# One decoder layer, expert part: how the gate matrix is made, and which tiles of product one stay on chip to open product two

## The chip, the cores and the metric

One core of one Trainium2 chip. The metric is the time of one execution in microseconds of device time; lower is better. Arithmetic is float32, where matrix products are made of three products of a value split into a high part (float32r) and a remainder (high times high, high times remainder, remainder times high).

## The reference, cut to what matters

A decoder layer on 512 tokens of width 1024: a mixer (RWKV and dilated attention), and then PEER, a layer of 16384 experts. Only the last part is touched. Per token and head (8 heads) two searches over 128 keys each give 16 best scores `v1, v2` with their key numbers `i1, i2`; the 16 best sums of a pair give 16 experts with softmax gates:

```python
cand = (v1[..., :, None] + v2[..., None, :]).reshape(cshape)          # 16 x 16 sums
cidx = (i1[..., :, None] * 128 + i2[..., None, :]).reshape(cshape)    # expert number
top, sel = lax.top_k(cand, 16);  idx = take_along_axis(cidx, sel)
gate = softmax(top)
act = gelu(einsum('cd,ced->ce', u, peer_u[idx]))                      # product one
out = einsum('ce,ced->cd', gate * act, peer_v[idx])                   # product two
```

## The kernel before, in words

The first 128 tokens (block 0) and the other 384 (blocks 1 to 3) go different ways.

**The 384 tokens** are computed densely. Product one (`phase_peer`, the loop at L1197) runs over 128 tiles `i1` of 128 experts: `gemm_ch` (L145) loads the tile's weights `uT` (512 KB, SP queue), splits them into `whi` (ScalarE, L127) and `wlo` (VectorE, L128), and makes 24 matmuls of 384 columns (L141 to L143); ScalarE applies Gelu (L1203) and the result `act` (128 experts x 384 tokens) is stored to DRAM (L1205, ScalarE's queue), but for the last 8 tiles, which stay on chip in `keep`. There are four pairs of weight buffers (two pools of two), so weights are ready some three tiles ahead.

**The gates** must become a dense matrix G of expert by token. `topk` (L1046) finds candidates, positions (VectorE max, find, replace) and the expert numbers: for each head a comparison, a product and a sum over 16 x 50 elements (L1076 to L1079), with the candidate numbers `cidx` made on GpSimd (L1056); for blocks 1 to 3 the number is then split by shift and mask (L1098 to L1104) and turned by three TensorE transposes into `sl`. `scatter` (L1113) goes through a block in 32 steps of four tokens: a one-hot E for the low part of the number (VectorE, L1122, 512 elements), four one-hots A for the high part times the gate (VectorE, L1126, 128 elements each), four matmuls E by A into one PSUM bank (L1132; the trace shows two passes for each, 8 records a step), and an eviction to `Gs` (ScalarE, L1133). After eight steps `Gs` (2 MB) goes to DRAM (`g_d`, L1135). `routing` (L1170) strings the four yields of one topk and the scatters of three blocks together; the loop of product one takes 10 + (i1 - 9) * 96 / 104 of its steps by tile i1, so that the program has the last of the 106 steps at tile 113; the rest, if any, is run at tile 119, where the pool of the routing (`pp`) is closed and the pool `vg` opened.

**The 128 tokens of block 0** are gathered: `rows_u` (L1144) fetches row after row of `peer_u` by an indirect DMA issued on GpSimd (L1141, 512 KB for 128 tokens, six buffers) and makes the dot product on VectorE (L1150, 1024 elements), one per tile of product one; `rows_v` (L1158) does the same with `peer_v` in product two (VectorE, L1164), into `acc0`.

**Product two** (L1232) runs over the 128 tiles again: the kept ones first, then the others, whose `act` is loaded again (L1243, SP queue). For every eight tiles a slab of G is loaded (L1235, 1.5 MB, from all twelve blocks of `g_d`). Each tile: act times G (VectorE, L1244), high part (ScalarE, L1250), remainder (VectorE, L1251), the weights `v` (512 KB) split as above, 18 matmuls of 512 columns into six PSUM banks. At tile 64 the program loads `h` (2 MB) and `gt2` (0.5 MB) for the end. The last four tiles are gone through output by output, so that the end can be pipelined.

**Order.** The program gives each piece a place by the `yield`s of these generators, but the order of the instructions on each engine is found when the kernel is built, by a scheduler that runs a model of the time (`schedule_with_timeline_sim`): an instruction with a later place in the program can be put ahead, when its inputs and its buffer are free. On the chip each engine, and each DMA queue, keeps the order that it was given.

Of the kernel before, what the change touches and what calls it, by code (L numbers as in the profile page):

```python
# [18 lines left out]
P = 128  # L19
# [25 lines left out]
GI = 8  # L45
# [55 lines left out]
class Kern:  # L101
# [942 lines left out]
    def topk(self, pp, i, res):  # L1044
# [5 lines left out]
        nc.vector.tensor_scalar(xf[:, :, 0], xf[:, :, 0], 128.0, None, op0=OP.mult)  # L1050
        cand = pp.tile([P, 8, NCAND], F32, tag="cand", name="cand")
        cidx = pp.tile([P, 8, NCAND], F32, tag="cidx", name="cidx")
        for p, (o, n) in enumerate(CAND):
            nc.vector.tensor_tensor(cand[:, :, o:o + n], v[:, :, 0, p:p + 1].to_broadcast([P, 8, n]),
                                    v[:, :, 1, 0:n], op=OP.add)
            nc.gpsimd.tensor_tensor(cidx[:, :, o:o + n], xf[:, :, 0, p:p + 1].to_broadcast([P, 8, n]),  # L1056
                                    xf[:, :, 1, 0:n], op=OP.add)
# [15 lines left out]
        xs = pp.tile([P, 8, 16], F32, tag="xs", name="xs")  # L1073
        for h in range(8):
            eq = pp.tile([P, 16, NCAND], F32, tag="eq", name="eq", bufs=2)
            nc.vector.tensor_tensor(eq, self.iota[:, None, :NCAND].to_broadcast([P, 16, NCAND]),  # L1076
                                    posf[:, h, :, None].to_broadcast([P, 16, NCAND]), op=OP.is_equal)
            nc.vector.tensor_tensor(eq, eq, cidx[:, h, None, :].to_broadcast([P, 16, NCAND]), op=OP.mult)
            nc.vector.tensor_reduce(xs[:, h], eq, axis=AX.X, op=OP.add)  # L1079
            if h % 2:  # L1080
                yield
# [8 lines left out]
        if i == 0:  # L1090
            xi = self.gp.tile([P, 8, 16], I32, name="xi0")
            nc.vector.tensor_copy(xi, xs)
# [5 lines left out]
        xi = pp.tile([P, 8, 16], I32, tag="xi", name="xi")  # L1098
        x2 = pp.tile([P, 8, 16], I32, tag="x2", name="x2")
        nc.vector.tensor_copy(xi, xs)  # L1100
        nc.vector.tensor_scalar(x2, xi, 127, None, op0=OP.bitwise_and)
        nc.vector.tensor_copy(sel[:, 1], x2)
        nc.vector.tensor_scalar(x2, xi, 7, None, op0=OP.logical_shift_right)
        nc.vector.tensor_copy(sel[:, 0], x2)  # L1104
# [8 lines left out]
    def scatter(self, pp, i, res):  # L1113

        nc = self.nc
        sl = res[i]
        for t4 in range(0, 128, 4):
            if t4 % GB == 0:
                Gs = pp.tile([P, 128, GB], F32, tag="Gs", name="Gs", bufs=2)
            E = pp.tile([P, 4, 128], F32, tag="ohE", name="ohE", bufs=2)  # L1120
            A = pp.tile([P, 4, 128], F32, tag="ohA", name="ohA", bufs=2)
            nc.vector.tensor_tensor(E, self.iota[:, None, :].to_broadcast([P, 4, 128]),  # L1122
                                    sl[:, 1, t4:t4 + 4, None].to_broadcast([P, 4, 128]), op=OP.is_equal)
            for j in range(4):
                t = t4 + j
                nc.vector.tensor_scalar(A[:, j], self.iota, sl[:, 0, t:t + 1], sl[:, 2, t:t + 1],  # L1126
                                        op0=OP.is_equal, op1=OP.mult)
            o = t4 % GB
            tg = "cdef"[t4 // 4 % 4]
            g = self.psum.tile([P, 4, 128], F32, tag=tg, name="gps", bufs=BANKS[tg])  # L1130
            for j in range(4):
                nc.tensor.matmul(g[:, j], E[:, j], A[:, j], start=True, stop=True)  # L1132
            nc.scalar.activation(Gs[:, :, o:o + 4].rearrange("p i t -> p t i"), g, AF.Copy)  # L1133
            if o == GB - 4:
                nc.scalar.dma_start(self.g_d[((i - 1) * 128 + t4) // GB], Gs)  # L1135
            yield
# [44 lines left out]
    def phase_peer(self, es):  # L1181
# [7 lines left out]
        self.iota = pp.tile([P, 128], F32, name="iota")  # L1189
# [6 lines left out]
        done = 0  # L1196
        for i1 in range(128):  # L1197
# [6 lines left out]
            if i1 < 128 - NR:  # L1204
# [12 lines left out]
        order = list(range(128 - NR, 128)) + list(range(128 - NR))  # L1217
# [4 lines left out]
        rows = self.rows_v(acc0)  # L1222
        LAST = 4
# [8 lines left out]
        for n, i1 in enumerate(order):  # L1232
            if n % GI == 0:
                G = vg.tile([P, TD // GB, GI, GB], F32, tag="G", name="G", bufs=2)
                nc.sync.dma_start(G, self.g_d[:, :, i1:i1 + GI, :].rearrange("b p i t -> p b i t"))  # L1235
# [3 lines left out]
            if i1 in keep:  # L1239
                act = keep[i1]  # L1240
            else:
                act = ap.tile([P, TD], F32, tag="act", name="act", bufs=4)
                nc.sync.dma_start(act, self.act_d[i1])  # L1243
            nc.vector.tensor_tensor(act.rearrange("p (b t) -> p b t", t=GB), act.rearrange("p (b t) -> p b t", t=GB),  # L1244
                                    G[:, :, n % GI, :], op=OP.mult)
            bufs = LAST if n >= 128 - LAST else 3
            tg = "f" if n >= 128 - LAST else ""
            wh = (vp if tg else vg).tile([P, TD], F32R, tag="wh" + tg, name="wh", bufs=bufs)
            wl = (vp if tg else vg).tile([P, TD], F32R, tag="wl" + tg, name="wl", bufs=bufs)
            nc.scalar.activation(wh, act, AF.Copy)  # L1250
            nc.vector.tensor_tensor(wl, act, wh.bitcast(F32), op=OP.subtract)  # L1251
            hi, lo = self.wtile(I["v"][i1 * 128:(i1 + 1) * 128, :])
            ws = (wh, wl, hi, lo)
# [22 lines left out]
def host(inputs):  # L1276
# [44 lines left out]
    a["iota"] = np.tile(np.arange(128, dtype=np.float32), (128, 1))  # L1321
# [17 lines left out]
```

## Time and profile before

| what | us |
|---|---|
| median of three runs (2125.58 to 2130.1) | 2126.97 |
| the profiled execution's own time | 2125.92 |
| its span in the trace | 2124.1 |
| product one with the scatters, in the trace | about 927 to 1561 |
| product two, in the trace | 1582.7 to about 2110 |

The span starts at the first instruction; the execution's own time has 1.8 us around it. TensorE is busy in 95% of the span, VectorE 75%, ScalarE 44%, GpSimd 30%. PEld is TensorE's loading of weights, which runs beside its matmuls. A granted clock of 1.00 is 2.4 GHz, 0.50 would be 1.2 GHz.

### The profile page before, as it was taken

To read this page: it belongs to the slowest core of one execution; us is meant where nothing else is said; L and a number is where in the kernel's file an instruction comes from. 1 tells how busy PE (TensorE), PEld (TensorE's weight loads), DVE (VectorE), ACT (ScalarE), POOL (GpSimd) and SP (SyncE) were. 2 spreads that over 40 slices of the span, in tenths; PEclk is the share of its full clock that TensorE was granted. 3 is DMA by queue.
4 is the path that set the end of the run, shared out by engine and by line. 5 is a ranking of instruction groups with operands and counts; after the bars stand their busy time and mean duration, and the time that the engine had idled before them with its cause. 6 is when DMAs were issued, how large, how long until landed. Compare 5 with 4: busy or idle time off the path is not lost.

```text
span 2124.1 us, 34025 instructions
## 1 busy us (share of the span) xinstructions
PE 2022.2 (95%) x12529; PEld 1744.0 (82%) x12529; DVE 1600.9 (75%) x3192; ACT 935.8 (44%) x1452; POOL 642.8 (30%) x511
## 2 busy tenths in 40 slices
PE   5999899999999998999999999999959999999999
PEld 4677667877877786899998999999958887877887
DVE  7466894853534555899999999987768898988555
ACT  3756665543324443334334454456633333333332
POOL 2424550221402111001674545420015555551000
PEclk9999989998889998999999999999979999999999
DMA  6666855354435532335998999985589999999763
GB/s 260 224 189 201 256 170 149 94 189 147 140 121 173 186 127 72 108 119 173 386 360 293 334 359 349 375 316 203 198 292 358 388 392 398 394 391 344 230 211 110
DMA packets 236299, 519.45 MB, mean 245 GB/s; under 512 B 35554, under 2 KB 129506, under 8 KB 233572
## 3 DMA queue, kind: packets, MB, share of 16 engines
q1 hardware_dynamic: 180260, 334.27, 46.4%
q0 software_dynamic: 36864, 134.23, 16.9%
q10 hardware_dynamic: 19008, 48.77, 6.0%
q8 instruction: 99, 1.62, 0.3%
q14 instruction: 68, 0.56, 0.1%
HBM read 432.23 MB, written 84.97 MB: 243 GB/s over the span
## 4 chain that ended last, share of the span: by engine, by line
PE 65%; DVE 16%; DMA 10%; issue 4%; ACT 3%; POOL 2%; SPq 0%; DVEq 0%; ACTq 0%; POOLq 0%
PE ps_mm L141 13%; PE ps_mm L143 13%; PE ps_mm L142 13%; DVE wlo L128 4%; PE gps L1132 4%; DMA wraw<-in_v 3%; DMA act<-act_d 2%; DVE row L1150 2%; PE yp L735 2%; PE yp L733 2%; PE ps_a L143 1%; PE ps_a L142 1%; PE ps_a L141 1%; DMA wada<-in_wada 1%; DVE acc L1164 1%
## 5 line engine op out<-in xcount | busy, mean ns | idle before, releaser
L127 ACT ACTIVATE whi<-wraw 128x1024 fp32r<-128x1024 f32 x356 | 370.1, 1042 | 388.6 <-PE ps_mm L142 226.9
L128 DVE TENSOR_TENSOR wlo<-wraw,whi 128x1024 fp32r<-128x1024 f32 x356 | 430.4, 1212 | 131.5 <-ACT whi L127 127.8
L141 PE MATMUL ps_mm<-n2h,whi 128*128 128x384 f32 (+1 forms) x1152 | 399.9, 347 | 3.2 <-ACT act L1203 3.2
L142 PE MATMUL ps_mm<-n2l,whi 128*128 128x384 f32 (+1 forms) x1152 | 398.2, 346 | 0.0
L143 PE MATMUL ps_mm<-n2h,wlo 128*128 128x384 f32 (+1 forms) x1152 | 396.1, 345 | 2.1 <-DVE wlo L128 2.1
L1141 POOL DMA_INDIRECT row<-in_v,xi x128 | 196.7, 1537 | 339.7 <-DVE acc L1164 166.5
L1141 POOL DMA_INDIRECT row<-in_u,xi x128 | 187.0, 1461 | 171.3 <-DVE dots L1150 132.7
L141 PEld LDWEIGHTS ps_mm<-n2h,whi 128*128 128x128 f32 x1152 | 218.4, 190 | 9.1 <-ACT act L1203 4.4
L143 PEld LDWEIGHTS ps_mm<-n2h,wlo 128*128 128x128 f32 x1152 | 218.2, 190 | 7.7 <-DVE wlo L128 2.8
L142 PEld LDWEIGHTS ps_mm<-n2l,whi 128*128 128x128 f32 x1152 | 218.3, 190 | 4.7
L141 PE MATMUL ps_mm<-n1h,whi 128*128 128x512 f32 x464 | 193.8, 421 | 8.8 <-ACT n1h L271 5.0
L143 PE MATMUL ps_mm<-n1h,wlo 128*128 128x512 f32 x464 | 192.5, 415 | 1.2 <-DVE wlo L128 1.2
L142 PE MATMUL ps_mm<-n1l,whi 128*128 128x512 f32 x464 | 192.4, 415 | 0.2 <-DVE n1l L272 0.2
L1250 ACT ACTIVATE wh<-act 128x384 fp32r<-128x384 f32 x128 | 66.9, 525 | 279.1 <-DVE act L1244 144.4
L1164 DVE SCALAR_TENSOR_TENSOR acc<-row,g,acc 128x1024 f32<-128x1024 f32 x127 | 162.3, 1278 | 0.8
L1150 DVE CUSTOM_DVE_ANT_0 row<-row,n2t 128x1024 f32<-128x1024 f32 x128 | 153.0, 1218 | 0.0
L1244 DVE TENSOR_TENSOR act<-act,G 128x384 f32<-128x384 f32 x128 | 69.8, 553 | 87.1 <-DMA act<-act_d 72.6
L1133 ACT ACTIVATE Gs<-gps 128x512 f32<-128x512 f32 x96 | 107.1, 1120 | 57.8 <-PE gps L1132 55.8
L141 PE MATMUL ps_mm<-whi,wh 128*128 128x512 f32 x256 | 92.6, 395 | 29.2 <-ACT wh L1250 29.0
L141 PEld LDWEIGHTS ps_mm<-n1h,whi 128*128 128x128 f32 x464 | 91.1, 198 | 32.5 <-ACT n1h L271 5.0
L143 PEld LDWEIGHTS ps_mm<-n1h,wlo 128*128 128x128 f32 x464 | 91.5, 197 | 23.0 <-DVE wlo L128 2.2
L142 PEld LDWEIGHTS ps_mm<-n1l,whi 128*128 128x128 f32 x464 | 92.1, 198 | 21.7 <-issue 2.4
(405 smaller groups left out, 4000.6 us busy)
## 6 DMA issues: line engine op xcount, KB each, us to landing
wraw<-in_uT SPq DMA_DIRECT2D x128, 512.0 KB
wraw<-in_v SPq DMA_DIRECT2D x128, 512.0 KB
wraw<-in_win SPq DMA_DIRECT2D x60, 512.0 KB
g_d<-Gs ACTq DMA_DIRECT2D x12, 2048.0 KB
G<-g_d SPq DMA_DIRECT2D x16, 1536.0 KB
act_d<-act ACTq DMA_DIRECT2D x120, 192.0 KB
act<-act_d SPq DMA_DIRECT2D x120, 192.0 KB
wada<-in_wada SPq DMA_DIRECT2D x64, 256.0 KB
```

What stands on the lines that cost most here:

```text
L127: nc.scalar.activation(hi[:, :n], raw[:, :n], AF.Copy)
L128: nc.vector.tensor_tensor(lo[:, :n], raw[:, :n], hi[:, :n].bitcast(F32), op=OP.subtract)
L141: mm(acc, lh, rh, start=start, stop=False)
L142: mm(acc, lh, rl, start=False, stop=False)
L143: mm(acc, ll, rh, start=False, stop=stop)
L1132: nc.tensor.matmul(g[:, j], E[:, j], A[:, j], start=True, stop=True)
L1133: nc.scalar.activation(Gs[:, :, o:o + 4].rearrange("p i t -> p t i"), g, AF.Copy)
L1141: self.nc.gpsimd.indirect_dma_start(row, None, self.I[tab], bass.IndirectOffsetOnAxis(ap=self.xi[:, n:n + 1], axis=0))
L1150: self.gathered(self.rowp, n, "u", lambda row: nc.vector.tensor_tensor_reduce(out=row, in0=row, in1=self.n2t, scale=1.0, scalar=0.0, op0=O ...
L1164: nc.vector.scalar_tensor_tensor(acc, row, self.gates0[:, n:n + 1], acc, op0=OP.mult, op1=OP.add)
L1244: nc.vector.tensor_tensor(act.rearrange("p (b t) -> p b t", t=GB), act.rearrange("p (b t) -> p b t", t=GB), G[:, :, n % GI, :], op=OP.mult)
L1250: nc.scalar.activation(wh, act, AF.Copy)
```

## The change

Four things in the expert part:

- **Gates into one-hots on ScalarE.** One comparison makes both one-hots A and E of a step (1024 elements, VectorE), and the four products of A with the gate are made by ScalarE (an ACTIVATE of 128 elements with the gate as a scale per partition). The one-hots have three buffers for two.
- **Indices by row and column.** The position in the list of 50 candidates is turned into a row (a sum of steps `dx` between row numbers, over comparisons with the 16 row offsets) and a column (position minus row offset), for two heads at a time, on 32 x 16 elements. `cidx` and GpSimd's part in it fall away, as do shift and mask; the table `iota` has the offsets and their differences behind its 128 numbers.
- **Scatter paced to end sooner** (96 / 98 steps a tile for 96 / 104, closing at tile 112 for 119), and 7 gathered rows of `rows_u` in 8 tiles for one a tile; the other 16 come in the first 17 tiles of product two, and `rows_v` after them, at 1.28 a tile.
- **The first 8 tiles stay on chip** and product two takes the tiles in their order. The first slab of G is loaded at tile 112 of product one, and three of the kept tiles are weighed (times G, split) at tiles 120, 122 and 124. The outputs go in the order of banks (2, 3, 1).

```diff
-        nc.vector.tensor_scalar(xf[:, :, 0], xf[:, :, 0], 128.0, None, op0=OP.mult)
+        dx = pp.tile([P, 8, 16], F32, tag="dx", name="dx")
+        nc.vector.tensor_copy(dx[:, :, 0:1], xf[:, :, 0, 0:1])
+        nc.vector.tensor_tensor(dx[:, :, 1:], xf[:, :, 0, 1:], xf[:, :, 0, :15], op=OP.subtract)
...
-            nc.gpsimd.tensor_tensor(cidx[:, :, o:o + n], xf[:, :, 0, p:p + 1].to_broadcast([P, 8, n]),
-                                    xf[:, :, 1, 0:n], op=OP.add)
...
-        for h in range(8):
-            eq = pp.tile([P, 16, NCAND], F32, tag="eq", name="eq", bufs=2)
-            nc.vector.tensor_tensor(eq, ..., op=OP.is_equal)
-            nc.vector.tensor_tensor(eq, eq, cidx[:, h, None, :].to_broadcast([P, 16, NCAND]), op=OP.mult)
-            nc.vector.tensor_reduce(xs[:, h], eq, axis=AX.X, op=OP.add)
+        for h0 in range(0, 8, 2):
...
+            nc.vector.tensor_tensor(ge, ph[:, :, None].to_broadcast([P, n, 16]), row(128), op=OP.is_ge)
+            nc.vector.tensor_tensor(by_head(eq), by_head(ge), dx[:, hs, None, :].to_broadcast([P, 2, 16, 16]), op=OP.mult)
+            nc.vector.tensor_reduce(sel[:, 0, hs].rearrange("p h k -> p (h k)"), eq, axis=AX.X, op=OP.add)
+            nc.vector.tensor_tensor(ge, ge, row(144), op=OP.mult)
+            off = pp.tile([P, n], F32, tag="off", name="off", bufs=2)
+            nc.vector.tensor_reduce(off, ge, axis=AX.X, op=OP.add)
+            nc.vector.tensor_tensor(off, ph, off, op=OP.subtract)
+            nc.vector.tensor_tensor(eq, off[:, :, None].to_broadcast([P, n, 16]), row(0), op=OP.is_equal)
+            nc.vector.tensor_tensor(by_head(eq), by_head(eq), xf[:, hs, 1, None, :].to_broadcast([P, 2, 16, 16]), op=OP.mult)
+            nc.vector.tensor_reduce(sel[:, 1, hs].rearrange("p h k -> p (h k)"), eq, axis=AX.X, op=OP.add)
+            yield
...
-            E = pp.tile([P, 4, 128], F32, tag="ohE", name="ohE", bufs=2)
-            A = pp.tile([P, 4, 128], F32, tag="ohA", name="ohA", bufs=2)
-            nc.vector.tensor_tensor(E, ..., op=OP.is_equal)
+            AE = pp.tile([P, 2, 4, 128], F32, tag="ohAE", name="ohAE", bufs=3)
+            A, E = AE[:, 0], AE[:, 1]
+            nc.vector.tensor_tensor(AE, self.iota[:, None, None, :128].to_broadcast([P, 2, 4, 128]),
+                                    sl[:, 0:2, t4:t4 + 4, None].to_broadcast([P, 2, 4, 128]), op=OP.is_equal)
             for j in range(4):
-                nc.vector.tensor_scalar(A[:, j], self.iota, sl[:, 0, t:t + 1], sl[:, 2, t:t + 1],
-                                        op0=OP.is_equal, op1=OP.mult)
+                nc.scalar.activation(A[:, j], A[:, j], AF.Copy, scale=sl[:, 2, t:t + 1])
...
+        def load_g(i1):
+            G = Gs[i1] = vg.tile([P, TD // GB, GI, GB], F32, tag="G", name="G", bufs=2)
+            nc.sync.dma_start(G, self.g_d[:, :, i1:i1 + GI, :].rearrange("b p i t -> p b i t"))
+        def weigh(i1, act):
+            nc.vector.tensor_tensor(act..., act..., Gs[i1 - i1 % GI][:, :, i1 % GI, :], op=OP.mult)
...
+            nc.scalar.activation(wh, act, AF.Copy)
+            nc.vector.tensor_tensor(wl, act, wh.bitcast(F32), op=OP.subtract)
+            ready[i1] = wh, wl
...
-            if i1 < 128 - NR:
+            if i1 >= NR:
                 act = ap.tile([P, TD], F32, tag="act", name="act", bufs=4)
...
-            next(rows, None)
-            while done < min(i1 + 1, 10) + max(i1 - 9, 0) * 96 // 104:
+            if i1 % 8 < 7:
+                next(rows, None)
+            while done < min(i1 + 1, 10) + max(i1 - 9, 0) * 96 // 98:
...
-            if i1 == 119:
+            if i1 == 112:
                 run(bg)
                 e1.close()
                 vg = self.pool(es, "vg")
-        run(rows)
+                load_g(0)
+            elif i1 >= 120 and i1 % 2 == 0 and len(ready) < 3:
+                weigh(len(ready), keep[len(ready)])
...
-        order = list(range(128 - NR, 128)) + list(range(128 - NR))
...
-                for t in out:
+                for t in (2, 3, 1):
...
-            next(rows, None)
-            if n > 64:
-                next(rows, None) if n % 16 == 0 else None
-        run(rows)
+            if n < 17:
+                next(rows, None)
+            while vdone < max(n - 16, 0) * 128 // 100:
+                next(rows_v, None)
+                vdone += 1
+        run(rows_v)
```

## Rows read from the trace of the kernel before

**Rows 1.** The profile's page, its first part: busy time, share of the span and count of instructions of each engine.
```profile
PE 2022.2 (95%) x12529; PEld 1744.0 (82%) x12529; DVE 1600.9 (75%) x3192; ACT 935.8 (44%) x1452; POOL 642.8 (30%) x511
```
**Rows 2.** Busy time by stage: the stretch, its length, busy time (and instructions) of PE, PEld, DVE, ACT, POOL, the granted clock, the DMA engines' share and GB/s.
```profile
1119.00:1407.00 288.00, 283.23 (x1721) 281.81 (x1720) 281.44 (x575) 136.02 (x167) 135.59 (x103) 0.98 0.94 344
1407.00:1561.00 154.00, 152.16 (x1028) 151.75 (x1026) 118.11 (x289) 94.78 (x105) 2.61 (x2) 1.00 0.59 209
1561.00:1582.00 21.00, 0.10 (x1) 0.00 (x0) 6.33 (x6) 1.07 (x1) 5.84 (x5) 0.55 0.97 347
1582.00:2110.00 528.00, 519.48 (x2265) 427.17 (x2266) 420.24 (x507) 188.53 (x252) 182.49 (x117) 0.99 0.90 329
```
**Rows 3.** The same view, 40 us of product one ahead of the scatters, and twice 40 us of product two.
```profile
1000.00:1040.00 40.00, 40.00 (x232) 40.00 (x232) 40.00 (x117) 13.55 (x19) 27.26 (x31) 1.00 0.92 339
1600.00:1640.00 40.00, 40.00 (x178) 33.11 (x177) 35.99 (x40) 14.78 (x20) 20.61 (x16) 1.00 0.96 351
...
1840.00:1880.00 40.00, 36.37 (x154) 29.61 (x153) 33.86 (x40) 13.31 (x17) 20.46 (x13) 0.96 1.04 395
```
**Rows 4.** The chain that ended last, between the two products: start, length, what.
```profile
1561.14 1.08 ACT Gs L1133
1562.24 7.40 DMA g_d<-Gs
1569.72 11.81 DMA G<-g_d
1581.56 0.57 DVE act L1244
1582.15 0.53 ACT wh L1250
```
**Rows 5.** PE in order of time at the same place: start, length, engine, line, what, and in brackets the idle time ahead and what ended it.
```profile
1559.93 1.17 PE L1132 MATMUL gps<-ohA,ohE 128*128 128x128 f32 x8 [1.60 <-DVE ohA L1126]
1582.73 0.80 PE L141 MATMUL ps_mm<-whi,wh 128*128 128x512 f32 x1 [21.63 <-ACT wh L1250]
...
1587.10 0.40 PE L141 MATMUL ps_d<-whi,wh 128*128 128x512 f32 x1
```
**Rows 6.** PE in order of time: the first matmul of a tile of product one, one of the two steps of the scatter inside this tile, and the first matmul of the next tile.
```profile
1480.26 0.42 PE L141 MATMUL ps_mm<-n2h,whi 128*128 128x384 f32 x1
...
1484.16 1.05 PE L1132 MATMUL gps<-ohA,ohE 128*128 128x128 f32 x8
...
...
1486.21 0.42 PE L141 MATMUL ps_mm<-n2h,whi 128*128 128x384 f32 x1
```
**Rows 7.** DVE by line from 927 to 1561: line, operation, names, shapes, count, busy us, mean ns, idle time ahead.
```profile
L1150 DVE CUSTOM_DVE_ANT_0 row<-row,n2t 128x1024 f32<-128x1024 f32 x128 | 153.0, 1218 | 0.0
L1126 DVE TENSOR_SCALAR ohA<-iota,sl 128x128 f32<-128x128 f32 x384 | 106.7, 344 | 0.0
L1122 DVE TENSOR_TENSOR ohE<-iota,sl 128x512 f32<-128x512 f32 x96 | 65.8, 685 | 8.9 <-PE gps L1132 8.8
L1076 DVE TENSOR_TENSOR eq<-iota,posf 128x800 f32<-128x800 f32 x32 | 31.0, 981 | 0.0
```
**Rows 8.** DVE in order of time: two 1024-element operations in a row, and two steps of the scatter.
```profile
1107.57 2.35 DVE L128 TENSOR_TENSOR wlo<-wraw,whi 128x1024 fp32r<-128x1024 f32 x2
...
1545.33 0.69 DVE L1122 TENSOR_TENSOR ohE<-iota,sl 128x512 f32<-128x512 f32 x1
...
1546.96 0.69 DVE L1122 TENSOR_TENSOR ohE<-iota,sl 128x512 f32<-128x512 f32 x1
```
**Rows 9.** Busy time by stretch of the scatter's PSUM tile alone: PE, PEld and ACT (eight PE records, and one eviction, are a step).
```profile
1000.00:1400.00 400.00, 43.28 (x328) 42.53 (x328) 46.27 (x41) 0.99 0.94 347
1400.00:1556.00 156.00, 54.68 (x418) 53.97 (x419) 56.71 (x51) 1.00 0.62 223
```
**Rows 10.** Busy time by stretch of line 1203 alone (the Gelu of product one, one a tile, and five table loads).
```profile
920.00:1400.00 480.00, 55.26 (x106) 0.99 0.87 315
```
**Rows 11.** ACT by line from 927 to 1561, columns as in the DVE rows.
```profile
L127 ACT ACTIVATE whi<-wraw 128x1024 fp32r<-128x1024 f32 x128 | 135.2, 1063 | 174.7 <-PE ps_mm L142 139.6 <-DMA wraw<-in_uT 16.0 <-ACT act L1203 5.0
L1133 ACT ACTIVATE Gs<-gps 128x512 f32<-128x512 f32 x95 | 106.0, 1121 | 56.1 <-PE gps L1132 54.1
L1203 ACT ACTIVATE act<-ps_mm 128x384 f32<-128x384 f32 x128 | 61.8, 482 | 91.5 <-PE ps_mm L143 85.1 <-issue 3.7 <-DMA wraw<-in_uT 2.8
...
L1085 ACT ACTIVATE sel<-sel 128x128 f32<-128x128 f32 x4 | 1.2, 311 | 3.0 <-DVE sel L1084 3.0
```
**Rows 12.** ACT in order of time, at a place of the merge: an ACTIVATE of 512 elements with a constant as its scale, and one of the same size with a scale per partition.
```profile
794.52 0.63 ACT L979 ACTIVATE hsq<-hT 128x512 f32<-128x512 f32 x1
795.06 0.71 ACT L983 ACTIVATE hf<-hT,f 128x512 f32<-128x512 f32 x1
```
**Rows 13.** PE's waits, of product one (927 to 1561) and from the end of product one to the end of product two (1561 to 2110): who waited for whom, us in total, times, longest.
```profile
PE ps_mm L141 <- ACT act L1203: 3.2, 4, 1.7
...
PE ps_mm L141 <- ACT wh L1250: 29.0, 6, 21.6
```
**Rows 14.** SP's queue in order of time, between the products.
```profile
1574.14 6.04 SPq L1237 DMA_DIRECT2D hfin<-h_d  x1
```
**Rows 15.** The DMA view of 1561 to 2124: packets, bytes, mean rate.
```profile
DMA packets 78462, 182.38 MB, mean 324 GB/s; under 512 B 6176, under 2 KB 45600, under 8 KB 78297
```
**Rows 16.** One line in all the span: the accumulation of rows of block 0 in product two.
```profile
L1164 DVE SCALAR_TENSOR_TENSOR acc<-row,g,acc x127: 1270/1277/1287, 1561.9 to 1940.3; 128x1024 f32<-128x1024 f32 x127
```

More of the change, by code (lines that the diff above doesn't have):

```diff
@@ L1072, in topk @@
         sel = pp.tile([P, 3, 8, 16], F32, tag="sel", name="sel")
-        xs = pp.tile([P, 8, 16], F32, tag="xs", name="xs")
-        for h in range(8):
-            eq = pp.tile([P, 16, NCAND], F32, tag="eq", name="eq", bufs=2)
-            nc.vector.tensor_tensor(eq, self.iota[:, None, :NCAND].to_broadcast([P, 16, NCAND]),
-                                    posf[:, h, :, None].to_broadcast([P, 16, NCAND]), op=OP.is_equal)
-            nc.vector.tensor_tensor(eq, eq, cidx[:, h, None, :].to_broadcast([P, 16, NCAND]), op=OP.mult)
-            nc.vector.tensor_reduce(xs[:, h], eq, axis=AX.X, op=OP.add)
-            if h % 2:
-                yield
+        for h0 in range(0, 8, 2):
+            hs = slice(h0, h0 + 2)
+            n = 32
+            ge = pp.tile([P, n, 16], F32, tag="ge", name="ge", bufs=2)
+            eq = pp.tile([P, n, 16], F32, tag="eq", name="eq", bufs=2)
+            ph = posf[:, hs].rearrange("p h k -> p (h k)")
+            row = lambda o: self.iota[:, None, o:o + 16].to_broadcast([P, n, 16])
+            by_head = lambda x: x.rearrange("p (h k) j -> p h k j", h=2)
+            nc.vector.tensor_tensor(ge, ph[:, :, None].to_broadcast([P, n, 16]), row(128), op=OP.is_ge)
[9 more added lines that the diff above has]
+            yield
         ga = sel[:, 2]
@@ L1091, in topk @@
             xi = self.gp.tile([P, 8, 16], I32, name="xi0")
-            nc.vector.tensor_copy(xi, xs)
+            nc.vector.tensor_scalar(sel[:, 0], sel[:, 0], 128.0, None, op0=OP.mult)
+            nc.vector.tensor_tensor(sel[:, 0], sel[:, 0], sel[:, 1], op=OP.add)
+            nc.vector.tensor_copy(xi, sel[:, 0])
             g0 = self.gp.tile([P, 128], F32, name="g0")
@@ L1097, in topk @@
             return
[L1098 to L1104, printed above, removed]
         tp = self.ps("a")
@@ L1188, in phase_peer @@
         pp = self.pool(e1, "pp")
-        self.iota = pp.tile([P, 128], F32, name="iota")
+        self.iota = pp.tile([P, 160], F32, name="iota")
         nc.sync.dma_start(self.iota, I["iota"])
@@ L1196, in phase_peer @@
         done = 0
+        ready, Gs = {}, {}
+        LAST = 4
+        def load_g(i1):
+            G = Gs[i1] = vg.tile([P, TD // GB, GI, GB], F32, tag="G", name="G", bufs=2)
+            nc.sync.dma_start(G, self.g_d[:, :, i1:i1 + GI, :].rearrange("b p i t -> p b i t"))
+        def weigh(i1, act):
+            nc.vector.tensor_tensor(act.rearrange("p (b t) -> p b t", t=GB), act.rearrange("p (b t) -> p b t", t=GB),
+                                    Gs[i1 - i1 % GI][:, :, i1 % GI, :], op=OP.mult)
+            tail = i1 >= 128 - LAST
+            bufs, tg, pool = (LAST, "f", vp) if tail else (3, "", vg)
+            wh = pool.tile([P, TD], F32R, tag="wh" + tg, name="wh", bufs=bufs)
+            wl = pool.tile([P, TD], F32R, tag="wl" + tg, name="wl", bufs=bufs)
+            nc.scalar.activation(wh, act, AF.Copy)
+            nc.vector.tensor_tensor(wl, act, wh.bitcast(F32), op=OP.subtract)
+            ready[i1] = wh, wl
         for i1 in range(128):
             acc = self.gemm_ch(I["uT"][i1], KT, n2h, n2l)
-            if i1 < 128 - NR:
+            if i1 >= NR:
                 act = ap.tile([P, TD], F32, tag="act", name="act", bufs=4)
@@ L1203, in phase_peer @@
             nc.scalar.activation(act, acc[:, :TD], AF.Gelu)
-            if i1 < 128 - NR:
+            if i1 >= NR:
                 nc.scalar.dma_start(self.act_d[i1], act)
-            next(rows, None)
-            while done < min(i1 + 1, 10) + max(i1 - 9, 0) * 96 // 104:
+            if i1 % 8 < 7:
+                next(rows, None)
+            while done < min(i1 + 1, 10) + max(i1 - 9, 0) * 96 // 98:
                 next(bg, None)
                 done += 1
-            if i1 == 119:
+            if i1 == 112:
                 run(bg)
@@ L1221, in phase_peer @@
         acc0 = vp.tile([P, D], F32, name="acc0")
-        rows = self.rows_v(acc0)
-        LAST = 4
+        rows_v = self.rows_v(acc0)
+        vdone = 0
         def mms(t, f, ws, n):
@@ L1231, in phase_peer @@
         last = []
[L1232 to L1235, printed above, removed]
+        for n in range(128):
+            if n % GI == 0 and n not in Gs:
+                load_g(n)
             if n == 64:
@@ L1238, in phase_peer @@
                 nc.sync.dma_start(gt2, self.gt2_d)
[L1239 to L1253, printed above, removed]
+            if n not in ready:
+                act = keep.get(n)
+                if act is None:
+                    act = ap.tile([P, TD], F32, tag="act", name="act", bufs=4)
+                    nc.sync.dma_start(act, self.act_d[n])
+                weigh(n, act)
+            hi, lo = self.wtile(I["v"][n * 128:(n + 1) * 128, :])
+            ws = (*ready[n], hi, lo)
             if n < 128 - LAST:
-                for t in out:
+                for t in (2, 3, 1):
                     for f in range(2):
@@ L1320, in host @@
     a["v"] = f(w["peer_v"])
-    a["iota"] = np.tile(np.arange(128, dtype=np.float32), (128, 1))
+    o = np.array([o for o, _ in CAND])
+    a["iota"] = np.tile(np.concatenate([np.arange(128), o, np.diff(o, prepend=0)]).astype(np.float32), (128, 1))
     a["masks"] = f(np.concatenate(mask, axis=1))
```

3 lines of the change are left out of this document (removed).

## The prediction

> **What bounds the kernel now.** First the page: TensorE is busy 95% of the span, and no other engine comes near [rows 1]. So the question is where TensorE stands still or runs at its lower clock; work taken from another engine counts only there. The view by stage says where. In the last 154 us of product one TensorE is busy for 152.2 us at granted clock 1.00; in the 288 us before, 283.2 at 0.98; in product two 519.5 of 528 at 0.99; but between the two there are 21 us with 0.1 us of work and a clock of 0.55 [rows 2]. VectorE is full in the 288 us (281.4) and not behind them (118.1 of 154): it is what makes the scatter late.
>
> That product one's time is TensorE's own can be summed. A stretch without scatter holds 232 matmuls in 40 us, 0.172 us each, so 24 take 4.14 us; from one tile's first matmul to the next, with two scatter steps between, it is 5.95 us, so a step adds 0.905 us [rows 3, 6]. 128 tiles and 96 steps make 530 + 87 = 617 us of the 634 from 927 to 1561. A matmul of product two takes 40/178 = 0.225 us [rows 3], and 2304 make 518 of 528. The change touches none of these counts. What it can win is the gap, and up to some 12 us lost inside product one: 4.8 idle in the 288 us, 5.8 for a clock of 0.98 there (half speed in 4% of the time), 1.8 behind [rows 2].
>
> The gap itself is a chain: last scatter step at 1559.9, eviction 1.1, store of the last block 7.4, load of the first slab of G 11.8, product with G 0.6, high part 0.5, first matmul at 1582.7, after 21.6 us of waiting [rows 4, 5]. Eleven matmuls then take 4.4 us where 2.5 is the later pace, since the clock has fallen to 1.2 GHz: 1.9 lost; and TensorE waited 1.6 for the last one-hots [rows 5]. Together **25.1 us**.
>
> **The change, part by part.**
>
> Kept tiles, early slab, early weighing. The chain stays as it is, some 22 us long, but hangs no longer on the end of product one, if the last scatter step comes 22 us (five tiles) ahead of it. Does it? By the program's places the last step of routing falls at tile 107 (10 + 98 x 96/98 = 106), 21 tiles or 87 us before the end. But the program's places don't hold: by 1400 some 101 tiles were done, for which the program would have 84 steps, and the trace has 41 [rows 9, 10]. The scatter was 43 steps behind, because VectorE was full.
>
> VectorE. A step costs it 1.63 us before, start to start; afterwards one operation of 1024 elements, 1.14 us as two such in a row show [rows 8]: 96 x 0.49 = 47 us less. Sixteen dot products go to product two: 16 x 1.22 = 20 us [rows 7]. The search for the index is no gain: 96 operations of 800 elements at 0.98 (94 us) become 128 of 512 at 0.685 (88 us) and 16 small ones at about 0.2 [rows 7]. GpSimd's 64 additions end no chain that TensorE waits for: nothing. So 67 us less, and 36 idle at the end [rows 2] could be used: by VectorE alone the scatter could end near 1561 - 103 = 1458, by the program's places near 1474. Either is some 60 us earlier than the 1539 that is needed. VectorE then no longer holds the scatter up.
>
> ScalarE. The trace has no 128-element ACTIVATE with a scale per partition. One with constants takes 0.311 [rows 11]; at 512 elements the scale per partition makes 0.71 of 0.63, and neighbours overlap by 0.09 [rows 12]. So 0.31 + 0.08 = 0.39, or 0.30 in a row: 384 of them are 115 to 150 us, on an engine that is busy 0.47 to 0.62 in these stages [rows 2]. In a tile with s steps ScalarE works 1.06 + 0.48 + s x (4 x 0.30 + 1.12) = 1.54 + 2.32 s, TensorE 4.14 + 0.905 s: ScalarE is the longer one from s = 1.8. The program asks for 0.98 a tile, so I take 2 us of new waiting (some four waits like the longest of the four Gelu waits, 1.7 us, would make 7 [rows 13]); the bounds are nothing, and at two steps a tile by full durations (1.54 + 2 x 2.68 = 6.9 against 5.95) 48 x 0.95 = 46 us. I stay near the low end, since the program's pace is the nearest row's half. The Trainium skill (ScalarE: Activation LUTs, Rules for kernel authors) says that multiplications belong on VectorE and not on ScalarE. Per operation the trace agrees: VectorE's 0.344 includes the comparison. Were ScalarE made the bound by it, the sum would be that of the third rival below.
>
> Queues that the moved steps pass. The first slab's load now stands in SP's queue among the weight loads of product one: if `g_d` isn't written when SP comes to it, these stand behind it, and TensorE has three tiles (12 us) of weights in hand. Its 11.8 us of transfer meet a DMA share of 0.59 [rows 2, 4]: hidden. Three weighings are six VectorE operations and three of ScalarE, in VectorE's idle time: hidden. Stores of tiles 120 to 127 replace those of 0 to 7: nothing. `h` and `gt2` (2.5 MB) were loaded in the gap [rows 14]; now they and the second slab meet product two's opening, 2.5 MB at 395 GB/s [rows 3] = 6.3 us: I take 1.5, as weights are 12 us ahead; the bounds are 0 and 6.3. The 16 moved rows are 8.4 MB more in product two: 182.4 MB become 189 [rows 15], 478 us at that peak rate, of 528. TensorE's waits there were 29.0 - 21.6 = 7.4 us [rows 13], all while rows came in; a longer inflow adds 1 (0 to 7.4, twice as many). `rows_v` ended at 1940 [rows 16]; by its new places it ends at tile 116, near 2040, before the last outputs: nothing.
>
> VectorE's relief in the 288 us stretch may take part of the 12 us lost in product one: I take 3, bounds 0 and 12.
>
> **Sum:** -25.1 + 2 + 1.5 + 1 - 3 = -23.6 us. The profiled execution took 2125.9, so 2102.3; it lies 1 us under the median of the runs, so **2103**. Its own bounds: 2089 with all 12 us back and nothing new, 2117 with both DMA terms at their worst (6.3 + 7.4, and no relief).
>
> **The rivals.**
>
> *The scatter is still late* (or stands behind SP's or VectorE's order, which was fixed by a model of the time). For: in the last stretch only 51 steps went in 156 us, two a tile [rows 9], so 55 steps from 1400 on would still end at 1561. Against: VectorE had idle time there, and 67 us less to do. Part of the chain stays, half of the 25: 2115. If all of it stays, the change does nothing that it was made for: 2127, no difference.
>
> *DMA takes it back.* Product two already runs at 0.90 of the DMA engines [rows 2], the gap's 21 us carried 347 GB/s, and 16 more rows come. For it: tiles waited for `act` and `v` while rows came in. If TensorE lost 5% of a 430 us inflow, 21 us, for 2% before: 2124. Against: 478 us of traffic in 528.
>
> *ScalarE becomes the bound, and it is slower.* ScalarE is one queue in order: the Gelu that frees a PSUM bank and the split of the next weights stand behind the gate products of whichever steps were put ahead, and these wait for VectorE's comparison. If the scatter, late at first as before, is caught up at two or three steps a tile (three buffers allow three: 1.54 + 6.96 = 8.5 against TensorE's 6.86, x 32 tiles = 53 us), TensorE waits 0.7 to 1.6 us in each such tile: some 35 to 50 us, so 2103 + 35 = 2138 at the least. It is slower than before from 0.5 us a tile in 48 tiles. Against: one step a tile leaves ScalarE at 3.9 of 5.05 us.
>
> **How the numbers follow.** Forecast 0.70 (2103, 2089 to 2117); late scatter 0.11 (2115, one in four of it no change); DMA 0.08 (2124, mostly no change); ScalarE 0.11 (2138). A measurement of this kernel tells about 0.2% (4 us) from no change. Faster: 0.70 + 0.08 + 0.03 = 0.81; same: 0.03 + 0.05 = 0.08; slower 0.11. The range is 2087 to 2124: it leaves out the third rival and little at the low end.
>
> **What would show it.** Right: no TensorE idle time over 3 us between products, clock 1.00 there; the last scatter step before 1500; VectorE's step at one operation of 1.2 us; product two within 3 us of 528. Wrong: TensorE waits for Gelu or for `whi` by tens of microseconds in product one (ScalarE), a wait for G at the opening (late scatter), more waits for `act` or `v` later (DMA).

## The result, and the profile of the changed kernel

The changed kernel takes **2102.6 us** (median of four runs) and the kernel before, on the same chip, 2128.5: a ratio of 0.9882 (95% interval 0.9869 to 0.9896). Its profiled execution took 2103.1 us, 22.8 less than that of before. The forecast was 2103.

The profile's page first [rows 1]: VectorE has 53 us less work, ScalarE 98 more, and TensorE issues the same 12529 instructions.

```profile
PE 2020.8 (96%) x12529; PEld 1740.5 (83%) x12529; DVE 1547.6 (74%) x2847; ACT 1034.3 (49%) x1836; POOL 597.5 (28%) x447
```

Then the place between the products [rows 5]. In order of time on TensorE, product two's first matmuls (those that read `wh`) stand between tiles of product one, whose last matmul starts at 1562.7. No line has idle time in brackets:

```profile
1553.42 0.33 PE L143 MATMUL ps_mm<-n2h,wlo 128*128 128x384 f32 x1
1553.60 0.63 PE L141 MATMUL ps_a<-whi,wh 128*128 128x512 f32 x2
...
1554.29 0.39 PE L141 MATMUL ps_d<-whi,wh 128*128 128x512 f32 x1
1554.52 0.34 PE L141 MATMUL ps_mm<-n2h,whi 128*128 128x384 f32 x1
```

The stages [rows 2, 3], columns as there. The row with 0.10 us of work and a clock of 0.55 is gone. The 288 us stretch is full at clock 1.00, but ahead of it there is a new loss: 200 matmuls in 1000 to 1040, where before had 232. First the kernel before from 1000 to 1119, which no row above shows, then the changed kernel:

```profile
1000.00:1119.00 119.00, 118.54 (x683) 117.87 (x683) 118.72 (x227) 40.86 (x56) 80.89 (x76) 1.00 0.96 359
```
```profile
1000.00:1040.00 40.00, 36.45 (x200) 35.49 (x199) 40.00 (x118) 14.26 (x19) 28.18 (x18) 0.97 0.96 353
1000.00:1119.00 119.00, 113.85 (x646) 112.12 (x645) 118.77 (x264) 54.02 (x86) 63.30 (x45) 0.97 0.94 349
1119.00:1407.00 288.00, 287.97 (x1838) 287.64 (x1838) 272.67 (x408) 219.83 (x433) 123.18 (x85) 1.00 0.94 346
1407.00:1555.00 148.00, 145.88 (x908) 144.43 (x907) 73.46 (x75) 97.98 (x198) 5.23 (x4) 1.00 0.72 261
1555.00:2082.00 527.00, 520.38 (x2285) 426.43 (x2284) 423.62 (x504) 190.26 (x254) 173.90 (x122) 1.00 0.91 335
```

The scatter's PSUM tile alone [rows 9]: 66 of the 96 steps are done by 1400, where before had 41. The second fence is one line in all the span, with the starts of the first and the last matmul: the last one starts at 1477.2 (1560.8 before, where the step that it belongs to begins at 1559.9).

```profile
1000.00:1400.00 400.00, 75.18 (x532) 72.99 (x533) 74.03 (x66) 0.99 0.94 346
1400.00:1556.00 156.00, 34.44 (x239) 32.92 (x237) 32.31 (x30) 1.00 0.73 266
```
```profile
L1137 PE MATMUL gps<-ohAE x768: 270/275/377, 1097.9 to 1477.2; 128*128 128x128 f32 x192
```

VectorE and ScalarE by line from 927 to 1556 [rows 7, 11]. A step costs VectorE one operation of 1.22 us; an operation of the search, with 512 elements, costs it 0.68. The gate products take ScalarE 0.40 us each.

```profile
L1155 DVE CUSTOM_DVE_ANT_0 row<-row,n2t 128x1024 f32<-128x1024 f32 x128 | 154.1, 1212 | 0.0
L1128 DVE TENSOR_TENSOR ohAE<-iota,sl 128x1024 f32<-128x1024 f32 x96 | 115.9, 1218 | 15.9 <-PE gps L1137 15.1 <-ACT sl L1115 0.7
L1085 DVE TENSOR_TENSOR ge<-ge,iota 128x512 f32<-128x512 f32 x16 | 10.9, 680 | 0.0
```
```profile
L1132 ACT ACTIVATE ohAE<-ohAE,sl 128x128 f32<-128x128 f32 x384 | 121.0, 400 | 4.6 <-ACT act L1227 2.2 <-DVE dots L1155 1.2 <-DVE wlo L128 0.8
```

Eight of them in a row take 0.31 us each, as the chain of work that ended last shows:

```profile
1447.45 2.48 ACT ohAE L1132 x8
```

The Trainium skill (ScalarE: Activation LUTs, What ACT_TABLE_LOAD costs) gives 186 ns and 0.833 ns an element, 93 more for an operand per partition, and 93 of overlap in a row. By these figures 128 elements are estimated at 386 ns, and at 293 in a row; the trace, with 400 and 310, agrees within 20.

TensorE's waits [rows 13], from 927 to 1556 and then from 1540 to 2090. The 21.6 us are gone; of the rest, nothing is longer than 2.1.

```profile
PE ps_mm L141 <- ACT act L1227: 4.4, 4, 2.1
PE gps L1137 <- ACT ohAE L1132: 2.4, 5, 0.7
PE ps_mm L143 <- DVE wlo L128: 0.4, 1, 0.4
```
```profile
PE ps_a L141 <- ACT wh L1217: 6.6, 15, 1.3
```

The first slabs of G, in SP's queue [rows 4, 14], are loaded at 1489, 12 us behind the last step and 64 ahead of product two. In VectorE's order the weighing of the kept tiles (times G) follows as soon as the slab lands, of all eight and not only of the three that the program put there.

```profile
1489.14 1.61 SPq L1207 DMA_DIRECT2D G<-g_d  x2
```
```profile
1498.49 3.84 DVE L1211 TENSOR_TENSOR act<-act,G 128x384 f32<-128x384 f32 x8 [6.31 <-DMA G<-g_d]
```

Two more lines, of the rows [rows 7, 16]: all 128 dot products of `rows_u` still fall into product one, and `rows_v` ends at 1923, earlier than before, not at 2040.

```profile
L1155 DVE CUSTOM_DVE_ANT_0 row<-row,n2t x128: 1197/1214/1220, 1007.7 to 1418.8; 128x1024 f32<-128x1024 f32 x128
```
```profile
L1169 DVE SCALAR_TENSOR_TENSOR acc<-row,g,acc x127: 1271/1278/1289, 1561.7 to 1922.6; 128x1024 f32<-128x1024 f32 x127
```

From the first matmul of product one to the last of product two it is 1193.7 us before (925.4 to 2119.1) and 1170.6 after (925.7 to 2096.3). The floor counted in the prediction is 617 + 518 = 1135, so by that count 36 us are still lost. Where they are is the second question of the experiments.

### The profile page after: what moved, and what is told of

Its sections match the earlier page's. It is cut to its first block, busy times and chain, and to the rows that moved or that the text cites. A ratio compares the mean times of both kernels' runs of the same rounds, so it can differ in the third digit from the quotient of the medians.

```text
span 2101.4 us, 33922 instructions
## 1 busy us (share of the span) xinstructions
PE 2020.8 (96%) x12529; PEld 1740.5 (83%) x12529; DVE 1547.6 (74%) x2847; ACT 1034.3 (49%) x1836; POOL 597.5 (28%) x447
## 4 chain that ended last, share of the span: by engine, by line
PE 70%; DMA 11%; DVE 8%; ACT 5%; issue 3%; POOL 1%; SPq 0%; ACTq 0%; DVEq 0%; POOLq 0%
PE ps_mm L141 15%; PE ps_mm L143 15%; PE ps_mm L142 15%; DMA act<-act_d 4%; PE gps L1137 3%; DVE wlo L128 2%; PE yp L735 2%; PE yp L733 2%; PE ps_a L141 2%; PE ps_a L142 2%; PE ps_a L143 2%; DMA G<-g_d 1%; DMA wraw<-in_v 1%; DMA wada<-in_wada 1%; DVE acc L1169 1%
## 5 line engine op out<-in xcount | busy, mean ns | idle before, releaser
L1146 POOL DMA_INDIRECT row<-in_v,xi x128 | 182.0, 1422 | 326.3 <-DVE acc L1169 163.4
L1128 DVE TENSOR_TENSOR ohAE<-iota,sl 128x1024 f32<-128x1024 f32 x96 | 115.9, 1218 | 15.9 <-PE gps L1137 15.1
L1132 ACT ACTIVATE ohAE<-ohAE,sl 128x128 f32<-128x128 f32 x384 | 121.0, 400 | 4.6 <-ACT act L1227 2.2
L1137 PE MATMUL gps<-ohAE 128*128 128x128 f32 x768 | 109.6, 276 | 2.4 <-ACT ohAE L1132 2.4
```

The costliest lines, as they stand in the source:

```text
L1128: nc.vector.tensor_tensor(AE, self.iota[:, None, None, :128].to_broadcast([P, 2, 4, 128]), sl[:, 0:2, t4:t4 + 4, None].to_broadcast([P, 2, ...
L1132: nc.scalar.activation(A[:, j], A[:, j], AF.Copy, scale=sl[:, 2, t:t + 1])
L1146: self.nc.gpsimd.indirect_dma_start(row, None, self.I[tab], bass.IndirectOffsetOnAxis(ap=self.xi[:, n:n + 1], axis=0))
```

## The experiments

First theory: the gap closes if the scatter's last step comes over 22 us before the end of product one, and what brings it forward is the work taken from VectorE. Rivals: the order (pacing, early slab, kept tiles) closes it; or a step's one-hot buffers do. Second theory: what is left is lost to gathered rows, whose DMAs delay the weights. All runs, with the ratio to the kernel before on the same chip, the scatter's steps by 1400, the start of its last matmul ("last step"), the start of product two, and the time between these two. The times inside a kernel are from its profiled execution:

| kernel | us | ratio (95%) | by 1400 | last step | product two | between |
|---|---|---|---|---|---|---|
| before | 2128.5 | 1 | 41 | 1560.8 | 1582.7 | 21.9 |
| changed | 2102.6 | 0.988 (0.987 to 0.990) | 66 | 1477.2 | 1553.6 | 76 |
| gates_only | 2106.0 | 0.990 (0.987 to 0.993) | 68 | 1495.3 | 1545.7 | 50 |
| order_only | 2122.3 | 0.998 (0.996 to 0.999) | 41 | 1564.1 | 1585.1 | 21.0 |
| vec_products | 2127.9 | 1.000 (0.998 to 1.001) | 42 | 1536.1 | 1555.7 | 19.6 |
| late_places | 2106.3 | 0.990 (0.988 to 0.992) | 68 | 1473.7 | 1549.0 | 75 |
| three_bufs | 2112.0 | 0.993 (0.989 to 0.996) | 59 | 1520.8 | 1554.3 | 34 |
| two_bufs | 2103.2 | 0.988 (0.985 to 0.990) | 55 | 1526.5 | 1548.9 | 22.4 |
| rows3 | 2092.2 | 0.981 (0.977 to 0.984) | 81 | 1475.4 | 1555.5 | 80 |
| vec_rows3 | 2109.2 | 0.989 (0.985 to 0.994) | 56 | 1545.7 | 1567.4 | 21.7 |
| changed_again | 2101.8 | 0.988 (0.986 to 0.989) | 66 | 1477.2 | 1553.5 | 76 |
| rows4 | **2079.2** | 0.978 (0.976 to 0.980) | 75 | 1465.7 | 1540.7 | 75 |
| before_rows3 | 2113.2 | 0.993 (0.990 to 0.995) | 54 | 1552.7 | 1573.3 | 20.6 |
| old_search | 2099.6 | 0.987 (0.985 to 0.989) | 63 | 1480.2 | 1548.7 | 69 |

The last column is the chain of [rows 4]. In the five kernels where TensorE waits between the products it is 19.6 to 21.9 us, whatever the cause of the late scatter; where it could be longer, there was no wait.

**gates_only**: the kernel before, with the changed search and scatter alone.
```diff
-            E = ...(ohE, bufs=2); A = ...(ohA, bufs=2)        # five VectorE operations a step
+            AE = pp.tile([P, 2, 4, 128], F32, tag="ohAE", name="ohAE", bufs=3)   # one, and four of ScalarE
...
```


> The kernel before with the new search for indices and the new scatter (one comparison on VectorE, gate products on ScalarE) alone; order of tiles, kept tiles, pacing and places as before. Theory (the gap was there because the scatter ended late, and it ended late because VectorE was full): VectorE has 47 us less to do, the last scatter step comes at 1500 or so, the first slab of G is loaded under product one, and TensorE waits under 3 us between the products: 2101 to 2108. Rival (the new order and pacing did it): the scatter is still paced to tile 113, the last tiles are the ones needed first, and 15 us or more of the gap stay: 2117 to 2127.


No wait between the products, and most of the gain: search and scatter are enough. The kernel still loses time in product two (2002 matmuls from 1590 to 2060, where before and changed have 2023).

**order_only**: the changed kernel with the search and scatter of before (the same diff, backwards).


> The changed kernel with the search for indices and the scatter of before (one-hots and gate products on VectorE); new order, kept tiles, pacing and early places. Theory: VectorE is as full as before, the last scatter step comes after 1530, and the chain of eviction, store, load of G and weighing (22 us) ends after product one does: 10 to 22 us of waiting, 2112 to 2128. Rival (order and pacing did it): 2101 to 2108.


The wait stays, though pacing, kept tiles and the early slab are all there:
```profile
1585.08 0.80 PE L141 MATMUL ps_a<-whi,wh 128*128 128x512 f32 x1 [20.70 <-ACT wh L1212]
```
Order, pacing and early places alone are worth 0.25% (0.09 to 0.42).

**vec_products**: the gate product back on VectorE, as one operation of 512 elements.
```diff
...
-                nc.scalar.activation(A[:, j], A[:, j], AF.Copy, scale=sl[:, 2, t:t + 1])
+            nc.vector.tensor_tensor(A, A, sl[:, 2, t4:t4 + 4, None].to_broadcast([P, 4, 128]), op=OP.mult)
```


> The changed kernel with the gate products back on VectorE: one product of 512 elements for the four ACTIVATEs of a step, so that a step costs VectorE 1.14 + 0.60 = 1.74 us, more than the 1.63 of before, and ScalarE has 115 us less. Theory (VectorE's relief was needed): as with the old scatter, last step after 1530, 2112 to 2130. Rival (order and pacing did it): 2101 to 2108. If ScalarE's waits cost anything in the changed kernel, the 2.4 us that TensorE waits for gate products there are gone here: no more than that below the changed kernel.


The whole gain is gone, but not in the way expected: 4.5 us of the gap came back, and the rest is lost in product two, where 102 matmuls fewer are done from 1590 to 2060 than in the changed kernel (23 us at 0.225). The three fences show the start of product two, that stretch, and TensorE's waits from 1590 to 2085:
```profile
1555.68 0.80 PE L141 MATMUL ps_a<-whi,wh 128*128 128x512 f32 x1 [4.53 <-ACT wh L1215]
```
```profile
1590.00:2060.00 470.00, 449.08 (x1921) 365.90 (x1920) 376.15 (x450) 159.82 (x215) 157.27 (x114) 0.98 0.94 340
```
```profile
PE ps_a L142 <- DVE wlo L128: 19.5, 9, 2.5
PE ps_a L141 <- ACT wh L1215: 1.4, 2, 0.8
```
Behind these waits are late weights (ScalarE waited 60.6 us for `wraw` in 1590 to 2060, in ten waits of up to 8.0). So the number was met for the wrong reason, and the second theory needed testing. The Trainium skill (ScalarE: Activation LUTs, Rules for kernel authors) puts multiplications on VectorE. Per operation that holds here: one product of 512 elements takes VectorE 0.68 us, four of 128 take ScalarE 1.24 in a row. For the kernel's time the measurement decides the other way, here and in vec_rows3 against rows3: VectorE was the fuller engine (280.5 us of the 288 from 1119 to 1407).

**late_places**: no early load of G and no early weighing, `rows_u` one a tile as before.
```diff
-            if i1 % 8 < 7:
-                next(rows, None)
+            next(rows, None)
...
-                load_g(0)
-            elif i1 >= 120 and i1 % 2 == 0 and len(ready) < 3:
-                weigh(len(ready), keep[len(ready)])
...
```


> The changed kernel, but the program's places are the late ones: the first slab of G is asked for at the start of product two, nothing is weighed ahead, and all 128 gathered rows of the first table have a place in product one (one a tile). Gates, order of tiles and pacing of the scatter are the new ones. Theory (the scheduler puts ahead what is ready; only the end of the scatter matters): the same time, 2100 to 2106. Rival (the early places count): the opening waits for the load of the slab, the weighing and the clock, 10 to 20 us: 2112 to 2122.


Nothing changes: the slab's load, which the program now has behind product one, is issued at 1484.7, against 1489.1 in the changed kernel. Its place in the program did not fix where it ran.

**three_bufs**: the kernel before, three buffers for each one-hot.
```diff
-            E = pp.tile([P, 4, 128], F32, tag="ohE", name="ohE", bufs=2)
+            E = pp.tile([P, 4, 128], F32, tag="ohE", name="ohE", bufs=3)
...                                                                  # and A alike
```


> The kernel before with three buffers for two for the one-hots E and A, and nothing else. Theory (two causes of the late scatter: VectorE full until 1407, and behind it the buffers, since two steps a tile is what two buffers give): 41 steps by 1400 as before, then three steps in a tile of 6.9 us, last step near 1535, chain of 22 us done when product one is: 0 to 5 us of waiting, 2104 to 2112. Rival (VectorE alone): last step after 1550 as before, 2120 to 2130.


The steps came otherwise than expected: 59 and not 41 by 1400, and the last at 1521. The wait is gone, with all of VectorE's old work. Some 60% of the gain (0.74 of 1.18%) come with it. Of the rest, some was paid in the 288 us stretch, where `wlo` now came late (7.4 us in four waits), and some in product two (1995 matmuls from 1590 to 2060 for 2023):
```profile
1119.00:1407.00 288.00, 277.94 (x1755) 276.10 (x1754) 287.56 (x630) 145.97 (x176) 117.83 (x89) 0.99 0.88 320
```

**two_bufs**: the changed kernel with two buffers (`bufs=3` to `bufs=2` for `ohAE`).


> The changed kernel with two buffers for three for the one-hots. Theory: VectorE's relief brings 60 steps or more by 1400; the other 30 at two a tile end near 1490, still 60 us ahead: 2100 to 2107, no waiting between the products. Rival (the third buffer did it): last step after 1530 and 10 us or more of waiting, 2112 to 2125.


The time is as expected, the steps are not: 55 by 1400 for 60, and the scatter ends at 1526 and not near 1490, 49 us later than with three buffers. That is just in time: `wh` is ready at 1546.8, and TensorE wants it at 1548.9. So either the relief of VectorE or the third buffer closes the gap; neither is needed beside the other.

**rows3**: three buffers for gathered rows in place of six, in the changed kernel.
```diff
-NUG = 6
+NUG = 3
```


> The changed kernel with three buffers for six for the gathered rows. Theory (what TensorE still waits in the products, 5 us and a fall of the clock at 1000 to 1119, and 6.6 us in product two, comes from weights and act that are late behind up to six rows, 3 MB, in flight): less waiting in both, 2092 to 2100. Rival (the waits come from the order on VectorE, or three buffers make the rows themselves late): 2101 to 2112.


0.7% less than the changed kernel, as expected, and no wait of TensorE is listed in 1590 to 2085.

**vec_rows3**: vec_products and `NUG = 3`.


> The kernel with the gate products back on VectorE, now with three buffers for six for the gathered rows. It lost its time not between the products (4.5 us) but in product two: 23 us of waiting and a fallen clock, once in about 36 us, when a slab of G (1.5 MB) and six rows delay a weight tile. Theory (DMA in flight): most of this goes, 2103 to 2113. Rival (order on VectorE, which stays): 2120 to 2132.


Product two has no wait any more, so what it lost in vec_products needed the six rows in flight. The gap is back, at nearly its full length, since the scatter ends at 1546 and product one now at 1548:
```profile
1567.38 0.79 PE L141 MATMUL ps_a<-whi,wh 128*128 128x512 f32 x1 [19.14 <-ACT wh L1215]
```

**changed_again**: the changed kernel, unedited, beside the next run.


> The changed kernel once more, as the measure for the three others on the same chip: 2100 to 2106.


The same time again; 1590 to 2060 is the row to compare:
```profile
1590.00:2060.00 470.00, 462.82 (x2020) 377.35 (x2019) 386.69 (x463) 169.06 (x224) 162.31 (x113) 1.00 0.94 346
```

**rows4**: the changed kernel with `NUG = 4`.


> The changed kernel with four buffers for six for the gathered rows. Theory (weights are late behind the rows in flight): between six and three buffers, 2091 to 2099, less waiting in product two than 6.6 us, and rows that end well ahead of the last outputs. Rival (only three are few enough, the DMA engines stay full with four): 2100 to 2106.


Better than expected, and faster than both kernels: 2.2% less than the kernel before, about 1% less than the changed one. The view of TensorE's waits lists none from 927 to 1590 and none from 1590 to 2085. By stage:
```profile
1000.00:1119.00 119.00, 118.92 (x704) 118.53 (x703) 117.55 (x272) 59.29 (x97) 50.80 (x39) 1.00 0.92 328
1119.00:1407.00 288.00, 288.00 (x1865) 287.90 (x1864) 273.88 (x393) 232.74 (x471) 116.33 (x78) 1.00 0.94 345
1407.00:1540.00 133.00, 133.00 (x823) 133.00 (x822) 74.30 (x86) 79.37 (x149) 21.16 (x15) 1.00 0.84 300
1590.00:2060.00 470.00, 470.00 (x2076) 389.18 (x2075) 388.91 (x466) 173.91 (x231) 158.08 (x111) 1.00 0.95 345
```
In the last row 56 matmuls more are done than in changed_again, 12.6 us at 0.225 [rows 3], though the idle times differ by 7.2 only: part of the loss lies in time that the profile counts as busy. Both products take 1144.2 us (927.3 to 2071.5), 26.4 less than in the changed kernel: 14.5 of it from product one's first matmul to product two's first, 11.9 behind.

**before_rows3**: the kernel before with `NUG = 3`.


> The kernel before with three buffers for six for the gathered rows, and nothing else. Theory: TensorE's waits for late weights go (7 us in product two, some of the 12 in product one), and rows that come more slowly leave VectorE to the scatter earlier, so that its end comes forward, though two buffers of one-hots allow two steps a tile: 2105 to 2119, part of the gap left. Rival (the rows cost only in the changed kernel, where the gap doesn't absorb them): 2123 to 2130.


As expected: part of the gap stays, product two is clean.
```profile
1573.33 0.80 PE L141 MATMUL ps_mm<-whi,wh 128*128 128x512 f32 x1 [13.01 <-ACT wh L1250]
```

**old_search**: the changed kernel with the index search of before (`topk` alone).


> The changed kernel with the search for indices of before (50-wide comparisons, candidate numbers on GpSimd, shift and mask). Theory (the new search costs VectorE what the old one did): 2100 to 2107, last scatter step before 1500. Rival (it was part of the relief): last step after 1515 and 2108 to 2118.


The intervals lie on one another: the search is worth nothing that can be measured in the whole. By stage it moves a loss: with the old search TensorE is busy for 117.9 of the 119 us from 1000 (114.7 in changed_again), but product two has 2006 matmuls for 2020.

## Why the prediction was right, point by point

- **The gap of 25.1 us**: right, and shown. It hung on the scatter's last step by a chain that measured 20 to 22 us in five kernels. No wait is left in any kernel whose scatter ended by 1527; vec_products, at 1536, waits 4.5, and before_rows3, at 1553, 13.0.
- **VectorE made the scatter late**: right, but not the whole cause. The last step was forecast for 1474 and came at 1477. Two buffers held the steps back as much as VectorE's load did: by 1400 the third buffer alone brings 59 steps for 41 (three_bufs), the lighter VectorE alone 55 (two_bufs), both 66; the prediction counted the third buffer only as room for ScalarE to fall behind. VectorE's step was put at 1.14 us and measures 1.22, and VectorE's work fell by 53 us and not by 67, as the dot products stayed.
- **Sixteen dot products to product two, 20 us**: this step failed. All 128 ran in product one: the scheduler orders them, and the place in the program did not move them, as late_places shows for the slab. The sum survived because the last step came 62 us earlier than the 1539 that was needed, and two_bufs, with its last step at 1526, shows that all but 13 us of these could be spared. In two_bufs itself 2 us were left, as TensorE there takes product two's first matmuls two tiles ahead of product one's end. `rows_v` until 2040 failed for the same reason.
- **ScalarE, +2**: right in size. 121 us in 384 products; TensorE waited 2.4 for one-hots, 1.4 of it before 1119. The Gelu waits, 3.2 before, are 4.4. The third rival's place exists: from 1407 to 1480 28 steps came beside 269 matmuls of product one (11 tiles), and ScalarE was full; but TensorE lost 1.1 us there, not 0.7 to 1.6 in each tile:
```profile
1407.00:1480.00 73.00, 71.94 (x485) 70.98 (x484) 47.27 (x46) 70.81 (x159) 5.23 (x4) 1.00 0.69 258
```
- **The opening, +1.5**: 0. The slab had landed 55 us before, and no wait in product two is over 1.3.
- **The inflow, +1**: 0. From 1590 to 2060 both kernels issue 2023 matmuls. There were no 16 more rows, as they never moved. The DMA rival's loss was there already and did not grow.
- **Relief in product one, -3**: about -2, as two larger terms. The 288 us stretch got its 4.8 idle and the clock's 5.8 back, some 10; but 1000 to 1119 now loses 5.2 idle and runs at 0.97, 3.6 more, where before was busy for 118.5 at 1.00. There the gathers start at 1001, and by 1040 TensorE has waited 3.1 us for two Gelus and 0.4 for a `wlo`. It takes six row buffers and the new search together: rows4 has 118.9 there, the four kernels with six buffers and the old search 117.9 to 118.5, the six with both 113.9 to 115.9. How the search does it is open. The 12 us also held 1.6 that the gap's 25.1 had counted already.

The terms for ScalarE and for the relief overlap, so they are better taken together. From 1000 to the end of the stages shown (1561 before, 1555 after), product one lost 11.3 us before (0.5 + 4.8 + 5.8 + 0.2, without the gap's 1.6) and 10.9 after (5.2 + 3.6 + 2.1), the waits for ScalarE included: -0.4, where +2 and -3 were forecast. That makes -25.1 - 0.4 = -25.5 against -22.8 in the two profiled executions. The remaining 3 us are not assigned; the two decimals of the clock alone leave some 2 open. So the gap was forecast with its cause, but that the sum met the time within 1 us is partly luck: the +2.5 for product two did not come, and about as much is unexplained.

What the prediction missed is what it took as given: product two's 528 us. Its own row of 154 matmuls in 40 us where others had 178 [rows 3] was a loss of 5.4 us in 40, but only the 7.4 us of listed waits were counted. In the changed kernel six row buffers in place of four cost some 23 us over both products (2101.8 against 2079.2), nearly what the change brought (26).

Open: why four buffers did better than three (the intervals of rows3 and rows4 overlap by 0.0025, and rows3's profiled run, its slowest, has 128.9 of 133 us busy behind 1407); why vec_products loses so much more in product two than the changed kernel, with the same six buffers and the same product two; and how much of order_only's 0.25% belongs to which of its parts.

## What to carry to other kernels

Measure a stall as a chain from the last producer to the first consumer, and ask by how much the producer must move: anything beyond brings nothing more, and several small means (a lighter engine, one more buffer) may each suffice. Count instructions done per stretch beside busy time and waits, since late data cost more here than the idle time showed. Where an engine prefetches into a ring of buffers, the number of buffers is also its pace: fewer can be faster when the DMA engines also carry what the bound engine needs.

## What the runs showed of the hardware

With six buffers for gathered rows of 512 KB the DMA engines' share is 1.03 or 1.04 while rows come in, with four mostly 0.97 to 0.99, and the bytes are the same (162.8 and 162.2 MB from 1590 to 2060). Product two in 40 us, the changed kernel and then rows4:

```profile
1720.00:1760.00 40.00, 38.30 (x166) 30.54 (x165) 36.78 (x42) 13.71 (x18) 20.67 (x16) 1.00 1.03 394
...
1960.00:2000.00 40.00, 40.00 (x178) 33.13 (x177) 21.35 (x29) 14.77 (x20) 0.00 (x0) 1.00 0.64 210
```
```profile
1720.00:1760.00 40.00, 40.00 (x178) 33.14 (x177) 32.24 (x39) 14.75 (x20) 13.05 (x10) 1.00 0.98 353
...
1960.00:2000.00 40.00, 40.00 (x178) 33.14 (x177) 33.26 (x41) 15.32 (x20) 14.91 (x10) 1.00 0.98 347
```

With six, 14 to 16 rows are fetched in 40 us until 1880, and the last is used at 1923; with four, about ten in 40 us, until 2046. From issue to landing a tile of `v` takes 9.3 us in the median with six and 7.3 with four, and a reloaded `act` 9.9 and 6.0; VectorE waited 67.3 us for `act` from 1590 to 2060 with six, and 2.2 with four. So DMA traffic at a rate lower by 10% went with a TensorE that was never late. The high rate alone is not enough for a loss: the kernel before has a share of 1.04 from 1680 to 1760, and all 178 matmuls in each 40 us.
